# A planner's lengths for the loading queue, and the order of an even mixer's query parts

## The chip, the cores and the metric

The kernel runs on one core of a Trainium2 chip. Its engines are TensorE (PE; its weight loads are shown apart as PEld), VectorE (DVE), ScalarE (ACT), GpSimd (POOL) and SyncE (SP), which here does nothing but issue DMA transfers. The metric is the device time of one execution in microseconds (us), as the median over runs.

## The reference

The program is an encoder trunk of two layers over 512 tokens of width 1024, with 256 memory tokens. Each layer has four steps, each followed by a layer norm: a half-step SwiGLU FFN, a token mixer, cross attention into the memory, and a second FFN.

```python
for i in range(DEPTH):
    j = i // 2
    y = swiglu(x, ffn_w_gate[i, 0], ffn_w_up[i, 0], ffn_w_down[i, 0])
    x = layer_norm(ALPHA * x + 0.5 * y, ln_g[i, 0], ln_b[i, 0])
    if i % 2 == 0:
        y = mixer_ab(x, ab_w_in[j], ab_w_out[j], ab_q_gain[j], ab_k_gain[j], ab_sink[j], ang_2d, ang_1d)
    else:
        y = mixer_c(x, c_w_in[j], c_w_out[j], c_rpb[j])
    x = layer_norm(ALPHA * x + y, ln_g[i, 1], ln_b[i, 1])
    y = memory_attn(x, mem, mem_w_q[i], mem_w_kv[i], mem_w_o[i])
    x = layer_norm(ALPHA * x + y, ln_g[i, 2], ln_b[i, 2])
    y = swiglu(x, ffn_w_gate[i, 1], ffn_w_up[i, 1], ffn_w_down[i, 1])
    x = layer_norm(ALPHA * x + 0.5 * y, ln_g[i, 3], ln_b[i, 3])
```

The even mixer (layer 0) has eight heads of dense attention with rms-normed, rotated queries and keys, and eight heads of attention in a window of 128 tokens to either side, with a learned sink. Heads are 64 wide, and four query heads share a key head. The odd mixer (layer 1) has 16 heads of attention in a two-dimensional neighbourhood with a bias per offset. Everything is float32.

## The kernel before

**Products.** Float32 operands are split in two parts of a narrower type (`fp32r`): a high part, which ScalarE makes as a cast, and a low part, which VectorE makes as the operand minus the high part. A product is three matmuls into one PSUM bank: high by high, high by low, low by high. So nearly everything that TensorE takes needs one ScalarE and one VectorE instruction first, in this order. Weights come through `weights`: SP loads them into one of two `raw` buffers, then the two engines split them into `slab` buffers. A third load into `raw` has to wait until the first buffer has been split.

**What sets the order.** The class `Graph` does not issue instructions as the program calls them. `record` stores each call as an `Op` with what it depends on. `emit` then plans twice: `plan` is a list scheduler over a model of the five engines and of two DMA queues (SP's and POOL's), with a cost in ns for each instruction (`cost`) and a length for each transfer. The first pass takes ready instructions in the order in which they were recorded. `deadlines` goes back through that order and gives every DVE, ACT and POOL instruction a due time; the second pass takes those as keys, while PE and SP keep the recorded rank. The instructions are issued in the order of the second pass, and on the chip each engine works through its own in that order, waiting where an operand isn't there. The model's times are thus not the chip's; they decide only who stands before whom. Since one length in the model changes the time of everything that follows, a changed length can swap instructions far from any transfer.

In the model a transfer on SP begins 1200 ns after its issue has ended, and not before the one ahead of it has ended; it takes 1650 ns for each 512 KB. A PSUM bank is held by one engine at a time in the model, reads included (`info["bank"]` in `record`).

**The even mixer's queries.** `queries` turns the queries of a pair of heads so that features lie on partitions, in one bank `ps`: partitions 0 to 63 are the one head, 64 to 127 the other. Each head's operand is a buffer of 128 partitions whose one half holds the high part and whose other half the low part. So a pair needs two ACT instructions (high parts) and two DVE instructions (low parts), each on 64 partitions; they are recorded ACT, DVE, ACT, DVE, and stand in the order of one instruction each for the pairs.

**The even mixer's end.** The output weights `ab_w_out` are loaded in `w_rows_pairs`, as two transfers to 64 partitions each. The last two loads (raw_1107 and raw_1112) take whole rows. The second of them goes into the `raw` buffer that held the memory tokens (raw_1080, from `memory_tokens`, called after head 13 of 16), which are split into four `slab` buffers for the memory attention that follows.

**The odd mixer.** Scores of a pair of heads are matmuls on a buffer `slab` that holds high and low parts of two heads; SP copies the parts there from `t2` buffers (four transfers of 128 KB for each buffer: two with high parts, two with low parts). PE interleaves the scores (`a`) with the values times probabilities of the pair before (`d`).

In names such as slab_1086_1167 below, the first number counts buffers through the program; the texts name a buffer by it. All instructions have the line of the call in `Op` (L156, and L157 after the change); a profile names buffers without numbers.

## Time and profile before

| | us |
|---|---|
| median of 3 runs (lowest to highest) | 2132.85 (2131.11 to 2132.93) |
| the profiled execution, whole | 2131.03 |
| its span, from the first to the last instruction | 2129.3 |
| PE busy | 2112.0 (99%) |
| PEld busy | 1870.6 (88%) |
| DVE busy | 1735.8 (82%) |
| ACT busy | 1161.7 (55%) |
| POOL busy | 285.1 (13%) |
| mean granted TensorE clock | 0.998 |

Outside the span lie 1.73 us of the profiled execution, and it is 1.82 us under the median. A busy time is the sum of an engine's instructions; matmuls overlap, since the end of one is modelled and the next has already begun, so a PE that is shown as 99% busy can still start its matmuls some tenths late. Whether it does is seen in the distance between starts. In a timeline a row is a run of like instructions: its start, its time to the end of the last, engine, line, operation, what it writes and reads, its shape, how many there are, and in square brackets how long the engine had been idle before it and what ended that. In the chain, each piece is what the next had to wait for.

### The profile page before, as it was taken

What the parts mean: (1) busy time and instruction counts of PE and PEld (TensorE: products, weight loads), DVE (VectorE), ACT (ScalarE), POOL (GpSimd) and SP (SyncE); (2) the same over time, 40 slices, a digit from 0 to 9 for tenths busy, and PEclk for the clock granted to TensorE, in tenths of its full rate; (3) what the DMA queues carried; (4) which work ended last, traced back from release to release, by engine and by line L of the source; (5) the groups of instructions that cost most, each with busy time, mean ns of one, the idle gap of its engine ahead of it and who ended that gap; (6) DMA issues with size and microseconds to landing.
All of it is one profiled execution on the core that took longest, in us unless ns stands there. A gap on an engine that the chain in (4) does not pass through costs nothing.

```text
span 2129.3 us, 32714 instructions
## 1 busy us (share of the span) xinstructions
PE 2112.0 (99%) x12648; PEld 1870.6 (88%) x12648; DVE 1735.8 (82%) x2500; ACT 1161.7 (55%) x1903; POOL 285.1 (13%) x379
## 2 busy tenths in 40 slices
PE   9999999999999999999999999999999999999997
PEld 7999988888888899998889999888888888999996
DVE  7789989888848879998879999866568479699997
ACT  5555443798546554445545455457665465444552
POOL 0001015310002000000200000312210011000003
PEclk9999999999999999999999999999999999999999
DMA  6566562003433346564445556256454433456551
GB/s 204 143 165 140 139 191 91 20 18 106 140 134 109 88 114 185 150 157 130 140 106 141 129 139 187 76 149 160 118 164 157 139 91 98 109 149 155 141 151 60
DMA packets 208859, 275.92 MB, mean 130 GB/s; under 512 B 10688, under 2 KB 151616, under 8 KB 208704
## 3 DMA queue, kind: packets, MB, share of 16 engines
q1 hardware_dynamic: 175904, 221.14, 33.6%
q0 software_dynamic: 32512, 52.44, 14.0%
q8 instruction: 100, 1.64, 0.3%
q14 instruction: 55, 0.45, 0.1%
q10 hardware_dynamic: 288, 0.26, 0.0%
HBM read 259.12 MB, written 4.19 MB: 124 GB/s over the span
## 4 chain that ended last, share of the span: by engine, by line
PE 89%; DVE 1%; DMA 1%; ACT 1%; issue 1%; SPq 0%; DVEq 0%; POOL 0%; ACTq 0%
PE a L156 55%; PE d L156 21%; PE t L156 14%; DMA slab<-t 1%; ACT slab L156 1%; DVE slab L156 1%; SPq L156 0%; DVE x L156 0%; ACT t L156 0%; DMA raw<-ab_w_out 0%; DVE t L156 0%; DVE xl L156 0%; DVEq L1657 0%; ACT xh L156 0%; DVE nmu L156 0%
## 5 line engine op out<-in xcount | busy, mean ns | idle before, releaser
L156 DVE TENSOR_TENSOR slab<-slab,slab 128x1024 fp32r<-128x1024 f32 (+3 forms) x638 | 727.9, 1167 | 76.0 <-ACT slab L156 37.7
L156 ACT CAST slab<-slab 128x1024 fp32r<-128x1024 f32 (+2 forms) x498 | 472.1, 983 | 341.4 <-DVE slab L156 142.7
L156 PE MATMUL a<-slab,slab 128*128 128x256 f32 (+3 forms) x2320 | 567.6, 323 | 1.9 <-DMA slab<-t 1.2
L156 PE MATMUL a<-xh,slab 128*128 128x256 f32 (+2 forms) x2480 | 559.8, 315 | 0.1
L156 PE MATMUL d<-slab,slab 128*128 128x512 f32 (+2 forms) x1856 | 447.8, 381 | 0.8 <-DVE slab L156 0.8
L156 PEld LDWEIGHTS a<-slab,slab 128*128 128x128 f32 x2320 | 409.4, 190 | 41.7 <-ACT t L156 1.3
L156 PEld LDWEIGHTS a<-xh,slab 128*128 128x128 f32 x2480 | 416.4, 190 | 33.4 <-ACT slab L156 1.0
L156 PE MATMUL a<-raw,slab 128*128 128x256 f32 x2048 | 388.8, 283 | 1.1 <-DVE t L156 1.0
L156 PE MATMUL a<-xl,slab 128*128 128x256 f32 (+1 forms) x1240 | 389.7, 314 | 0.0
L156 PEld LDWEIGHTS d<-slab,slab 128*128 128x128 f32 x1856 | 328.9, 189 | 57.2 <-DVE slab L156 1.7
L156 PEld LDWEIGHTS a<-raw,slab 128*128 128x128 f32 x2048 | 327.8, 192 | 6.7 <-ACT slab L156 1.9
L156 PEld LDWEIGHTS a<-xl,slab 128*128 128x128 f32 x1240 | 236.3, 191 | 18.4
L156 PE MATMUL t<-slab,slab 128*128 128x512 f32 (+1 forms) x840 | 209.3, 389 | 0.0
L156 DVE TENSOR_TENSOR slab<-raw,slab 128x1024 fp32r<-128x1024 f32 (+2 forms) x140 | 159.6, 1157 | 23.3 <-ACT slab L156 23.2
L156 PEld LDWEIGHTS t<-slab,slab 128*128 128x128 f32 x840 | 149.9, 189 | 26.2
L156 DVE TENSOR_TENSOR slab<-t,slab 128x512 fp32r<-128x512 f32 (+2 forms) x223 | 137.5, 637 | 12.3 <-ACT slab L156 11.2
L156 ACT CAST slab<-t 128x512 fp32r<-128x512 f32 (+2 forms) x223 | 120.7, 567 | 41.4 <-DVE t L156 15.0
L156 ACT CAST slab<-raw 128x1024 fp32r<-128x1024 f32 (+1 forms) x132 | 123.7, 970 | 25.1 <-PE a L156 9.0
L156 ACT COPY t<-a 128x512 f32<-128x512 f32 (+1 forms) x116 | 63.5, 551 | 130.0 <-PE a L156 76.5
L156 DVE SCALAR_TENSOR_TENSOR x<-d,x 128x512 f32<-128x512 f32 x168 | 114.9, 686 | 16.8 <-PE d L156 16.1
L156 POOL DMA_DIRECT2D slab<-ffn_w_down x40 | 47.7, 1193 | 315.2 <-DVE slab L156 296.9
L156 DVE TENSOR_TENSOR t<-a,t 128x512 f32<-128x512 f32 (+2 forms) x99 | 61.0, 618 | 33.8 <-PE a L156 20.6
(126 smaller groups left out, 2143.0 us busy)
## 6 DMA issues: line engine op xcount, KB each, us to landing
slab<-ffn_w_gate SPq DMA_DIRECT2D x80, 512.0 KB
slab<-ffn_w_up SPq DMA_DIRECT2D x80, 512.0 KB
slab<-ffn_w_down SPq DMA_DIRECT2D x80, 512.0 KB
slab<-ffn_w_down POOLq DMA_DIRECT2D x40, 512.0 KB, 5.8
raw<-mem_w_kv SPq DMA_DIRECT2D x16, 1024.0 KB
slab<-t SPq DMA_DIRECT2D x96, 128.0 KB
slab<-ffn_w_gate POOLq DMA_DIRECT2D x16, 512.0 KB, 7.7
slab<-ffn_w_up POOLq DMA_DIRECT2D x16, 512.0 KB, 6.0
```

The lines of the kernel that those rows point to most:

```text
L156: op.call = lambda: fn(*args, **kw)
```

## The change

Two things are changed, both only in what the planner is told. First, the length of a transfer on SP's queue is now 250 ns and 1700 ns for each 512 KB (1950 for a transfer of 512 KB, where it was 1650), it begins 1040 ns after its issue has begun (where it was 1200 ns after the end of an issue of 600, so 1800), and it takes 1.7 times as long if it moves 512 KB or more into 64 partitions or fewer. That last case is only the two loads of `ab_w_out` in whole rows, four transfers of 512 KB. POOL's queue is as it was. Second, `queries` records both ACT parts and then both DVE parts, and the first DVE part depends on the second ACT part, so that the planner puts them in that order.

```diff
--- before.py
+++ after.py
@@ -40,7 +40,7 @@
 
 class Op:
     __slots__ = (
-        "engine", "adds", "ns", "call", "deps", "users", "wait", "ready", "end", "frees", "index", "rank", "dma", "size", "port", "table",
+        "engine", "adds", "ns", "call", "deps", "users", "wait", "ready", "end", "frees", "index", "rank", "dma", "size", "port", "table", "thin",
         "key", "start", "stop", "lands", "later",
     )
 
@@ -149,6 +149,7 @@
         func = args[2] if method == "activation" else None
         op.table = str(func) if func in (AF.Silu, AF.Exp) else None
         op.size = math.prod(outs[0].shape) * 4
+        op.thin = op.dma and engine == "sync" and op.size >= 2**19 and outs[0].shape[0] <= 64
         op.port = method in ("tensor_tensor", "scalar_tensor_tensor", "tensor_scalar") and (
             engine == "gpsimd" or engine == "vector" and math.prod(outs[0].shape[1:]) >= 64 and all(z.space != bass.MemoryType.PSUM for z in ins)
         )
@@ -254,8 +255,9 @@
             lands = stop + self.LATENCY[e]
             if op.dma:
                 kind = e == "sync"
-                work = op.size / 2**19 * (4000.0 if op.adds else 1650.0)
-                begin = max(stop + (1200.0 if kind else 2000.0), queues[kind][-1][1])
+                work = 250.0 + op.size / 2**19 * 1700.0 if kind else op.size / 2**19 * (4000.0 if op.adds else 1650.0)
+                work *= 1.7 if op.thin else 1.0
+                begin = max(t + 1040.0 if kind else stop + 2000.0, queues[kind][-1][1])
                 finish = begin + work + 0.5 * shared(queues[not kind][-6:], begin, begin + work)
                 queues[kind].append((begin, finish))
                 lands = finish + 790.0
@@ -1060,15 +1062,18 @@
             n = len(blocks) * P
             ps = self.transposed([(i * P, P, tiles[t][:, pr * P : (pr + 1) * P]) for i, t in enumerate(blocks)])
             both = both or self.pair()
-            for s, z in enumerate(both):
-                z = z[:, blocks[0] * P : blocks[0] * P + n]
-                own, other = slice(64 * s, 64 * s + 64), slice(64 - 64 * s, 128 - 64 * s)
-                shape = lambda y: y.rearrange("p (r c) -> p r c", r=ROWS) if natural else y
-                src = by_rows(ps[own, :n], natural)
-                nc.scalar.activation(shape(z[own]), src, AF.Copy, scale=-0.125)
+            own = lambda s: slice(64 * s, 64 * s + 64)
+            shape = lambda y: y.rearrange("p (r c) -> p r c", r=ROWS) if natural else y
+            src = [by_rows(ps[own(s), :n], natural) for s in range(2)]
+            z = [z[:, blocks[0] * P : blocks[0] * P + n] for z in both]
+            for s in range(2):
+                nc.scalar.activation(shape(z[s][own(s)]), src[s], AF.Copy, scale=-0.125)
+            for s in range(2):
                 nc.vector.scalar_tensor_tensor(
-                    out=shape(z[other]), in0=src, scalar=-0.125, in1=shape(z[own].bitcast(F32)), op0=ALU.mult, op1=ALU.subtract
+                    out=shape(z[s][own(1 - s)]), in0=src[s], scalar=-0.125, in1=shape(z[s][own(s)].bitcast(F32)),
+                    op0=ALU.mult, op1=ALU.subtract,
                 )
+            nc.ops[-2].deps.add(nc.ops[-3])
             return both
 
         def keys(tile_, natural):
```

No instruction, operand or buffer is added or taken away. Each engine has the same instructions in another order: about 100 of ACT's rows, 140 of DVE's and of PE's, 6 of POOL's and two pairs of SP's stand elsewhere. Of the even mixer's query parts both ACT instructions now stand together, and both DVE instructions behind them. Three other places follow.

ScalarE in the even mixer near its end. The rows `ACTIVATE t2,l<-t2,mn` are exponentials of scores, `ACTIVATE t2<-t2,l` the division by their sums, slab_1086 to slab_1092 the high parts of turned probabilities, and slab_1081 to slab_1084 those of the memory tokens raw_1080. Before:

```order
L156 ACTIVATE t2_1045_1126<-t2_1045_1126,l_1047_1128 128x384
L156 ACTIVATE t2_1049_1130<-t2_1049_1130,l_1051_1132 128x256
L156 ACTIVATE t2_1067_1148,l_1069_1150<-t2_1067_1148,mn_1068_1149 128x385
L156 ACTIVATE t2_1063_1144,l_1065_1146<-t2_1063_1144,mn_1064_1145 128x257
L156 CAST slab_1086_1167<-t_1085_1166 128x256
L156 CAST slab_1088_1169<-t_1087_1168 128x384
L156 CAST slab_1090_1171<-t_1089_1170 128x384
L156 ACTIVATE t2_1071_1152,l_1073_1154<-t2_1071_1152,mn_1072_1153 128x385
L156 CAST slab_1092_1173<-t_1091_1172 128x256
L156 CAST slab_1081_1162<-raw_1080_1161 128x2x256
L156 CAST slab_1082_1163<-raw_1080_1161 128x2x256
L156 CAST slab_1083_1164<-raw_1080_1161 128x2x256
```

After:

```order
L157 ACTIVATE t2_1049_1130<-t2_1049_1130,l_1051_1132 128x256
L157 CAST slab_1083_1164<-raw_1080_1161 128x2x256
L157 CAST slab_1084_1165<-raw_1080_1161 128x2x256
L157 CAST slab_1081_1162<-raw_1080_1161 128x2x256
L157 CAST slab_1082_1163<-raw_1080_1161 128x2x256
L157 CAST slab_1086_1167<-t_1085_1166 128x256
L157 CAST slab_1088_1169<-t_1087_1168 128x384
L157 CAST slab_1090_1171<-t_1089_1170 128x384
L157 ACTIVATE t2_1067_1148,l_1069_1150<-t2_1067_1148,mn_1068_1149 128x385
L157 CAST slab_1092_1173<-t_1091_1172 128x256
L157 ACTIVATE t2_1063_1144,l_1065_1146<-t2_1063_1144,mn_1064_1145 128x257
L157 ACTIVATE t2_1071_1152,l_1073_1154<-t2_1071_1152,mn_1072_1153 128x385
```

The four casts of the memory tokens now stand ahead of the casts of turned probabilities and of the three exponentials; VectorE's subtractions for them move ahead in the same way, between those for slab_1086 and slab_1088.

TensorE at the even mixer's output projection. d_1118 and a_1119 are two of its sums and d_1127 a third; slab_1113 and slab_1114 are the high and low part of the weights that were loaded as raw_1112. Before:

```order
L156 MATMUL d_1118_1199<-slab_1110_1191,slab_1026_1107 128x512
L156 MATMUL d_1118_1199<-slab_1113_1194,slab_1078_1159 128x512
L156 MATMUL d_1118_1199<-slab_1114_1195,slab_1078_1159 128x512
L156 MATMUL d_1118_1199<-slab_1113_1194,slab_1078_1159 128x512
L156 MATMUL d_1118_1199<-slab_1115_1196,slab_1103_1184 128x512
L156 MATMUL a_1119_1200<-slab_1111_1192,slab_1026_1107 128x512
L156 MATMUL d_1118_1199<-slab_1116_1197,slab_1103_1184 128x512
```

After:

```order
L157 MATMUL d_1118_1199<-slab_1110_1191,slab_1026_1107 128x512
L157 MATMUL d_1118_1199<-slab_1113_1194,slab_1078_1159 128x512
L157 MATMUL a_1119_1200<-slab_1111_1192,slab_1026_1107 128x512
L157 MATMUL a_1119_1200<-slab_1110_1191,slab_1026_1107 128x512
L157 MATMUL a_1119_1200<-slab_1113_1194,slab_1078_1159 128x512
L157 MATMUL d_1127_1208<-slab_1108_1189,slab_966_1047 128x512
L157 MATMUL d_1127_1208<-slab_1109_1190,slab_966_1047 128x512
L157 MATMUL d_1118_1199<-slab_1114_1195,slab_1078_1159 128x512
L157 MATMUL d_1118_1199<-slab_1113_1194,slab_1078_1159 128x512
```

Between the matmul of d_1118 on slab_1113 and the one on slab_1114 there now stand five matmuls of other sums.

TensorE in the odd mixer, at the scores of one pair of heads. a_2794 to a_2811 are banks of scores; of two matmuls into one the first reads the half of slab_2768 or slab_2769 that is copied first, the second the half that is copied second. d_2813 and d_2814 are values times probabilities, t_2824 the next product. Before:

```order
L156 MATMUL d_2813_2894<-slab_2773_2854,slab_2704_2785 128x2x128 x2
L156 MATMUL a_2805_2886<-slab_2769_2850,slab_2730_2811 128x192 x2
L156 MATMUL d_2814_2895<-slab_2775_2856,slab_2703_2784 128x256
L156 MATMUL a_2807_2888<-slab_2769_2850,slab_2730_2811 128x256 x2
L156 MATMUL d_2814_2895<-slab_2775_2856,slab_2703_2784 128x256
L156 MATMUL a_2809_2890<-slab_2769_2850,slab_2730_2811 128x256 x2
L156 MATMUL a_2811_2892<-slab_2769_2850,slab_2730_2811 128x192 x2
L156 MATMUL d_2814_2895<-slab_2775_2856,slab_2703_2784 128x256 x2
L156 MATMUL d_2814_2895<-slab_2777_2858,slab_2704_2785 128x256 x2
```

After:

```order
L157 MATMUL a_2805_2886<-slab_2769_2850,slab_2730_2811 128x192
L157 MATMUL d_2814_2895<-slab_2775_2856,slab_2703_2784 128x256
L157 MATMUL d_2814_2895<-slab_2777_2858,slab_2704_2785 128x256
L157 MATMUL a_2807_2888<-slab_2769_2850,slab_2730_2811 128x256
L157 MATMUL d_2814_2895<-slab_2777_2858,slab_2704_2785 128x256
L157 MATMUL a_2809_2890<-slab_2769_2850,slab_2730_2811 128x256
L157 MATMUL d_2814_2895<-slab_2777_2858,slab_2704_2785 128x2x128 x2
L157 MATMUL t_2824_2905<-slab_2818_2899,xh_2_83 128x512
L157 MATMUL a_2805_2886<-slab_2769_2850,slab_2730_2811 128x192
L157 MATMUL a_2807_2888<-slab_2769_2850,slab_2730_2811 128x256
L157 MATMUL a_2809_2890<-slab_2769_2850,slab_2730_2811 128x256
```

The second matmuls of a_2805, a_2807 and a_2809 now stand behind the first ones of all three, five of d_2814 and one of t_2824.

## The prediction

> **What bounds the kernel now.** I read the page's first and fourth part first (busy time, and the shares of the chain that ended last), then TensorE's waits, then the timelines of the places where the order of instructions differs. Page, parts 1 and 4:
>
> ```profile
> PE 2112.0 (99%) x12648; PEld 1870.6 (88%) x12648; DVE 1735.8 (82%) x2500; ACT 1161.7 (55%) x1903; POOL 285.1 (13%) x379
> ...
> PE 89%; DVE 1%; DMA 1%; ACT 1%; issue 1%; SPq 0%; DVEq 0%; POOL 0%; ACTq 0%
> ```
>
> The reader is to see that TensorE (PE) is the bound: 2112.0 of 2129.3 us, and 89% of the chain. No matmul is added or removed, so a new order can only give back time in which PE waits, or add such time. How much there is to give back stands in PE's waits, total us, times, longest:
>
> ```profile
> PE a L156 <- DMA slab<-t: 1.2, 3, 0.6
> PE t L156 <- DVE junk L156: 1.2, 1, 1.2
> PE a L156 <- DVE t L156: 1.0, 1, 1.0
> PE d L156 <- DVE slab L156: 0.8, 1, 0.8
> PE t L156 <- DVE x L156: 0.6, 1, 0.6
> ```
>
> These are the large ones; they come to 4.8 us. The row "DVE junk" is the start, and "DVE t" sits in the first FFN at 129 us, where the order is the same in both kernels; "DVE x" is the layer norm before the odd mixer, also unchanged. What the change can reach is the first row (the odd mixer's scores, which wait for copied query and key parts) and the fourth (one matmul in the even mixer's output projection). This view counts idle time after a matmul's modelled end. I therefore price a wait by starts: two starts on PE less the slot of the first. The slot is 0.23 us for 512 columns and 0.12 for 256, by these timeline rows (start, us busy; a row with x7 is seven matmuls from that start):
>
> ```profile
> 1049.39 0.39 PE L156 MATMUL a<-slab,xl 128*128 128x512 f32 x1
> 1049.62 0.39 PE L156 MATMUL a<-slab,xh 128*128 128x512 f32 x1
> ...
> 1528.67 1.02 PE L156 MATMUL d<-slab,slab 128*128 128x256 f32 x7
> 1529.53 0.25 PE L156 MATMUL a<-slab,slab 128*128 128x192 f32 x1
> 1530.38 0.33 PE L156 MATMUL a<-slab,slab 128*128 128x192 f32 x1 [0.60 <-DMA slab<-t]
> ```
>
> (1049.62 − 1049.39 = 0.23; (1529.53 − 1528.67)/7 = 0.12.)
>
> **Term 1, the late output weights of the even mixer (−1.0 us).** Rows of the chain, SP, ACT, DVE and PE timelines, in this order:
>
> ```profile
> 519.92 6.59 DMA raw<-ab_w_out
> ...
> 519.28 1.25 SPq L156 DMA_DIRECT2D raw<-ab_w_out  x2
> ...
> 526.61 2.00 ACT L156 CAST slab<-raw 128x1024 fp32r<-128x1024 f32 x2 [1.98 <-DMA raw<-ab_w_out]
> ...
> 527.70 2.36 DVE L156 TENSOR_TENSOR slab<-raw,slab 128x1024 fp32r<-128x1024 f32 x2 [1.50 <-ACT slab L156]
> ...
> 526.80 1.41 PE L156 MATMUL d<-slab,slab 128*128 128x512 f32 x5
> 528.98 0.50 PE L156 MATMUL d<-slab,slab 128*128 128x512 f32 x1 [0.76 <-DVE slab L156]
> ...
> 516.08 2.19 ACT L156 CAST slab<-raw 128x512 fp32r<-128x512 f32 x4
> ...
> 516.75 2.50 DVE L156 TENSOR_TENSOR slab<-raw,slab 128x512 fp32r<-128x512 f32 x4
> ```
>
> The buffer of raw_1112 is free only when DVE has split the memory tokens raw_1080 (516.75 + 2.50 = 519.25); SP issues the load at once (519.28), it lands 6.59 us after the second issue, ACT casts, DVE subtracts, and PE waits for that split: the last of the five starts at 526.80 + 4 × 0.23 = 527.72, the next matmul at 528.98, so 1.26 − 0.23 = 1.0 us are lost. Now the four casts stand right behind the last normalisation of the head before (512.77, see term 2). Each takes 0.52 of the queue (2.19 with the tail of the last), so they run from about 512.8 to 514.9, and the subtractions, between other work of DVE, are through near 517.0. The load is issued some 2.2 us earlier and lands near 524.3. Beside that PE has five other matmuls (5 × 0.23 = 1.15) between the one on the cast part and the one on the subtracted part. Either of the two covers the 1.0. Ends: −1.0 and 0; I take −1.0, since two covers would both have to fail.
>
> The Trainium skill ("SBUF — State Buffer", section "Door 1: The DMA port swizzle") gives 196 GB/s for a 1 MiB load into 64 partitions against 328 for 128. By that this load, which comes as two halves of 64 partitions, would take 1.05 MB / 196 GB/s = 5.4 us (an estimate), land 1.2 us sooner than the row shows, and PE would not wait for it even before; term 1 would be 0 and the sum 1.0 us smaller. The trace has 6.59 and the wait, so the measurement decides.
>
> **Term 2, what the earlier casts push back (+0.3).**
>
> ```profile
> 511.75 1.02 ACT L156 ACTIVATE t<-t,l 128x384 f32<-128x384 f32 x2
> 512.66 0.61 ACT L156 ACTIVATE t<-t,mn 128x385 f32<-128x385 f32 x1
> ...
> 514.14 1.19 ACT L156 CAST slab<-t 128x256 fp32r<-128x256 f32 x3 [0.28 <-PE t L156]
> ...
> 514.57 0.85 PE L156 MATMUL d<-slab,slab 128*128 128x256 f32 x3
> ```
>
> Behind those casts on ACT now stand the casts of the turned probabilities (slab_1086, 1088, 1090; before at 514.14) and the exponentials of the next heads (before at 512.66). The first cast ends about 4 × 0.52 + 0.37 after 512.7, at 515.1. PE wants it at 514.57, or at 514.80 now that one other matmul stands ahead: +0.3. The later parts have 0.2 to 0.3 us of room, since PE's new order puts three, then five matmuls of d_1094 between them. The exponentials end near 518.3 instead of 518.7, because ACT has the same work and only another order. Ends: 0, and +0.6 if the casts take 2.19 + 0.5.
>
> **Term 3, the odd mixer's scores (−1.2).** PE's timeline at two other places like the one at 1530.38 above:
>
> ```profile
> 1482.30 0.28 PE L156 MATMUL d<-slab,slab 128*128 128x256 f32 x1
> 1482.86 0.58 PE L156 MATMUL a<-slab,slab 128*128 128x192 f32 x3 [0.28 <-DMA slab<-t]
> ...
> 1484.61 0.39 PE L156 MATMUL t<-slab,xh 128*128 128x512 f32 x1
> 1485.10 0.33 PE L156 MATMUL a<-slab,slab 128*128 128x192 f32 x1
> ...
> 1551.95 0.30 PE L156 MATMUL d<-slab,slab 128*128 128x256 f32 x1
> 1552.28 0.33 PE L156 MATMUL a<-slab,slab 128*128 128x192 f32 x1
> 1552.90 0.33 PE L156 MATMUL a<-slab,slab 128*128 128x192 f32 x1 [0.30 <-DMA slab<-t]
> ```
>
> Lost: 1482.86 − 1482.30 − 0.12 = 0.44 and 1485.10 − 1484.61 − 0.23 = 0.26; 1530.38 − 1529.53 − 0.12 = 0.73; 0.33 − 0.12 = 0.21 and 0.62 − 0.12 = 0.50. The copies are issued by SP in the same order as before, so I leave their landings where they are and move only PE. At 1530 eight other matmuls (five of d_2814, two scores on the first half, one of the next product) now stand between the matmul on the first half and that on the second, which PE reaches at 1531.1, after the landing: −0.73. At 1552 three matmuls of 0.12 stand there: 0.50 becomes 0.14, −0.36. At 1482 the second halves stand directly behind the first ones, one matmul earlier than before: PE reaches them at 1482.23 and waits 0.63, after which nothing else is late: 0.63 instead of 0.70, −0.1. Sum −1.2; ends −1.5 (all of 1552 too) and 0.
>
> **Edits that I cost at nothing.** The query parts themselves: ACT's and DVE's rows of one of them.
>
> ```profile
> 402.47 0.58 ACT L156 ACTIVATE slab<-t 64x512 fp32r<-64x512 f32 x1
> ...
> 404.50 0.59 ACT L156 ACTIVATE slab<-t 64x512 fp32r<-64x512 f32 x1
> ...
> 403.79 0.68 DVE L156 SCALAR_TENSOR_TENSOR slab<-t,slab 64x512 fp32r<-64x512 f32 x1
> ...
> 405.15 0.69 DVE L156 SCALAR_TENSOR_TENSOR slab<-t,slab 64x512 fp32r<-64x512 f32 x1
> ```
>
> The second ACT part started 0.03 after DVE's first ended (403.79 + 0.68 = 404.47), so the four are done one after the other, 3.4 us from 402.47 to 405.84. Two behind two, they could be done in 2 × 0.58 + 2 × 0.68 = 2.5. PE's waits above have no row of 1 us or more on such a part, so other matmuls cover most of the chain, and shortening it by 3.4 − 2.5 = 0.9 gains a part of that at best: 0, ends −0.3 and +0.3 (a third of the 0.9, gained, or lost where another value is pushed behind a part).
>
> In the rms norm of the first query block the transpose of slab_532 moves up on PE from 376.39 to about 374.6, and POOL's addition that it needs took 373.43 to 375.82:
>
> ```profile
> 373.43 2.39 POOL L156 TENSOR_TENSOR slab<-t,t 128x512 f32<-128x512 f32 x1 [1.30 <-DVE t L156]
> ...
> 376.39 0.27 PE L156 MATMUL t<-ident,slab 128*128 128x128 f32 x1
> ```
>
> POOL waited 1.30 us there for DVE, whose rope work for this block now stands ahead of others, so I take 0; ends 0 and +1.2.
>
> At the start of the second layer's first FFN PE takes six matmuls on slab_1949 from 1049.85 on, 4.1 us before DVE had made it (1052.69 + 1.22 = 1053.91); but DVE too now makes it before the addition that stood at 1045.96:
>
> ```profile
> 1045.96 0.69 DVE L156 SCALAR_TENSOR_TENSOR x<-d,x 128x512 f32<-128x512 f32 x1
> ...
> 1052.69 1.22 DVE L156 TENSOR_TENSOR slab<-slab,slab 128x1024 fp32r<-128x1024 f32 x1
> ```
>
> There it starts by about 1046.4 and ends by 1047.6, 2.2 us ahead of PE; the addition behind it waits anyway, for sums that PE now ends 1.1 us later. 0. The two SP swaps (FFN weights near 18 and 830 us) and the casts that trade places inside the FFN bodies lie beside work that PE has queued, with no PE wait in those rows: 0, ends ±0.3 together.
>
> **Sum.** −1.0 + 0.3 − 1.2 = −1.9 against the profiled execution: 2131.03 − 1.9 = 2129.1 (span 2127.4). The profiled execution stands 1.8 under the median 2132.85, so as a median 2130.9. A change of 0.2% is 4.3 us, about what a measurement of this kernel can tell from no change; the forecast is well inside it.
>
> **Rivals.** (a) The waits come back one step later: PE reaches the next scores earlier and waits there for copies that have not moved. For it: DMA landings set these waits, not PE. Against: the copies of the next pair hang on products that PE then also makes earlier. It gives −1.9 + 1.2 + about 0.7, so 2132.8, no change. (b) The change does nothing that reaches PE, for instance because the earlier load meets other traffic and the PE fillers only shift the wait: 2132.5 to 2133.5, as in (a). (c) Slower: DVE comes late to slab_1949. One held instruction ahead of it on DVE that makes it end after 1049.85, so more than 2.2 us late, stops PE; at worst, with DVE as in the old order, it costs 4.06, and from 1.9 on the kernel is slower: 2132.85 − 1.9 + 4.06 = 2135.0. Against it: the instructions ahead of it wait for sums that PE ends by 1045.5. (d) Much faster, over 4.3 us: all of the rows above that the change can reach, 1.0 + 2.1, do not come to that, so only waits that I have not priced could.
>
> **How the numbers follow.** Forecast (−0.5 to −3.4) 0.56; (a) and (b) 0.16; (c) and other new waits of 1 to 4 us net 0.11; new waits of over 4.3 us net 0.08; (d) 0.09. The forecast's own range is 2129.5 to 2132.3. The range for 8 in 10 reaches to (c), 2135.0, and at the low side to −4.5, where the unpriced ends of every term meet (−1.0 − 1.5 − 0.3 − 0.3 and a run to run scatter of 1.8): 2128.4. Faster by over 0.2% is (d) and a little of the forecast's tail, 0.10; slower by over 0.2% is the new waits of over 4.3 us and a little of (c), 0.10; within 0.2% is 0.80.
>
> **What would show it.** Right: raw<-ab_w_out issued near 517 instead of 519.28, no PE row with DVE slab at 528, the PE wait on DMA slab<-t down from 1.2 to about 0.5 with the one at 1482 left, and a wait of 0.3 near 514.9. Wrong: a PE wait of over 1 us on DVE slab near 1050, on POOL slab near 375, or on ACT t near 519 to 521.

## The result, and the profile after

The changed kernel takes 2125.8 us (median of 7 runs, 2125.5 to 2127.03), the kernel before beside it 2132.05 (7 runs, 2130.44 to 2132.93): a ratio of 0.9973, 95% interval 0.9963 to 0.9982. By the ratio that is 5.8 us (3.8 to 7.9), where 1.9 were forecast, and the time lies below the range (from 2128.4 us). Ratios here and below are worked out from all runs, so what they give in us can differ by some tenths from the difference of two medians. The profiled execution took 2125.8 us, with a span of 2123.9 at the same granted clock (0.998).

The page of the changed kernel, busy times and the shares of the chain that ended last:

```profile
PE 2109.2 (99%) x12648; PEld 1871.0 (88%) x12648; DVE 1735.8 (82%) x2500; ACT 1161.2 (55%) x1903; POOL 287.4 (14%) x379
...
PE 96%; DVE 1%; ACT 1%; DMA 1%; issue 0%; SPq 0%; DVEq 0%; ACTq 0%
```

All engines do the same work as before; the chain now runs over PE for 96% of the span, where it was 89%. PE's waits (total us, times, longest):

```profile
PE t L157 <- DVE junk L157: 1.2, 1, 1.2
PE t L157 <- DVE x L157: 0.7, 1, 0.7
PE t L157 <- DVE slab L157: 0.4, 1, 0.4
PE a L157 <- DMA slab<-t: 0.4, 2, 0.2
PE a L157 <- DVE slab L157: 0.4, 1, 0.4
PE a L157 <- ACT slab L157: 0.3, 1, 0.3
```

Against the waits of before, four rows are gone or smaller: "DVE t" (1.0, the first FFN), "d <- DVE slab" (0.8, the output projection), "ACT t" (0.3, the even mixer) and "DMA slab<-t" (1.2, now 0.4; the three of before are gone, and two of 0.2 are new, at 1457.78 and 1570.75). They come to 2.9 us. Two rows are new: "t <- DVE slab" (0.4, at 485.87) and "ACT slab" (0.3, at 4.90). The rest of the gain is not in this view, since it counts only idle time after a modelled end.

So the two traces are compared by starts: the same instructions of PE at both ends of a stretch, at points where PE has done the same set of work in both. Each number is the length of that stretch after less its length before, in us; a second pair of traces of both kernels, taken later on one chip, stands beside it.

| stretch of before's trace | first pair | second pair |
|---|---|---|
| 1 to 30, first loads | −0.08 | −0.70 |
| 110 to 131, first FFN | −0.90 | −1.27 |
| 131 to 455 | −0.02 | −0.05 |
| 455 to 465, even mixer | −0.52 | −0.56 |
| 465 to 526 | +0.14 | +0.13 |
| 526 to 535, output projection | −1.49 | −1.52 |
| 535 to 1035 | +0.12 | −0.07 |
| 1035 to 1075, second layer's first FFN | −0.22 | −0.23 |
| 1075 to 1457 | −0.06 | −0.05 |
| 1457 to 1580, odd mixer | −1.93 | −1.79 |
| 1580 to 2118 | −0.27 | −0.48 |
| all | −5.2 | −6.6 |

There is no single place. Four stretches carry 4.8 of the 5.2 us in the first pair and 5.1 of the 6.6 in the second: the first FFN, one point of the even mixer, the output projection and the odd mixer.

**Output projection.** Rows of the changed kernel's timelines of SP, ACT, DVE and PE, in this order:

```profile
515.52 1.25 SPq L157 DMA_DIRECT2D raw<-ab_w_out  x2
...
511.03 2.17 ACT L157 CAST slab<-raw 128x512 fp32r<-128x512 f32 x4
...
523.09 2.00 ACT L157 CAST slab<-raw 128x1024 fp32r<-128x1024 f32 x2 [0.18 <-DMA raw<-ab_w_out]
...
524.36 0.68 DVE L157 SCALAR_TENSOR_TENSOR x<-d,x 128x512 f32<-128x512 f32 x1
524.96 2.35 DVE L157 TENSOR_TENSOR slab<-raw,slab 128x1024 fp32r<-128x1024 f32 x2
...
526.48 0.84 PE L157 MATMUL a<-slab,slab 128*128 128x512 f32 x3
527.15 1.30 PE L157 MATMUL d<-slab,slab 128*128 128x512 f32 x5
```

PE goes through without a wait. This part of the trace stands 1.3 us earlier than in before, for what was gained ahead of it; the load is issued 3.8 us earlier on the clock (519.28 to 515.52), so 2.4 earlier in its place, where 2.2 were forecast. Note the row at 524.36, DVE's addition ahead of the two subtractions; it turns out to matter.

**First FFN.** Before, DVE and PE:

```profile
113.81 1.23 DVE L156 TENSOR_TENSOR slab<-slab,slab 128x1024 f32<-128x1024 f32 x1 [1.49 <-DMA slab<-ffn_w_down]
114.95 0.69 DVE L156 TENSOR_TENSOR slab<-t,t 128x512 f32<-128x512 f32 x1
...
123.15 2.96 DVE L156 TENSOR_TENSOR slab<-slab,slab 128x1024 fp32r<-128x1024 f32 x3 [0.20 <-ACT slab L156]
...
129.80 0.36 PE L156 MATMUL a<-raw,slab 128*128 128x256 f32 x1 [1.03 <-DVE t L156]
```

After, DVE:

```profile
112.96 0.68 DVE L157 TENSOR_TENSOR slab<-t,t 128x512 f32<-128x512 f32 x1
113.57 1.22 DVE L157 TENSOR_TENSOR slab<-slab,slab 128x1024 f32<-128x1024 f32 x1
```

DVE waited 1.49 us for a down weight while the product behind it (114.95) was ready. Now the product stands first and fills that idle time. From there to PE's wait at 129.80 DVE's only idle time is the 0.20 us at 123.15, so what is done earlier at 113 arrives 15 us later at PE: that wait is gone.

### The profile page after: what moved, and what is told of

Its sections match the earlier page's. It is cut to its first block, busy times and chain, and to the rows that moved or that the text cites. A ratio compares the mean times of both kernels' runs of the same rounds, so it can differ in the third digit from the quotient of the medians.

```text
span 2123.9 us, 32745 instructions
## 1 busy us (share of the span) xinstructions
PE 2109.2 (99%) x12648; PEld 1871.0 (88%) x12648; DVE 1735.8 (82%) x2500; ACT 1161.2 (55%) x1903; POOL 287.4 (14%) x379
## 4 chain that ended last, share of the span: by engine, by line
PE 96%; DVE 1%; ACT 1%; DMA 1%; issue 0%; SPq 0%; DVEq 0%; ACTq 0%
PE a L157 59%; PE d L157 23%; PE t L157 15%; DVE slab L157 1%; ACT t L157 1%; DMA slab<-t 1%; DVE x L157 0%; ACT slab L157 0%; SPq L157 0%; DVE t L157 0%; DMA raw<-x_t 0%; ACT xh L157 0%; DVE mn L157 0%; DVE xl L157 0%; DVEq L1662 0%
## 5 line engine op out<-in xcount | busy, mean ns | idle before, releaser
L157 ACT ACTIVATE t<-a 128x512 f32<-128x512 f32 (+3 forms) x65 | 36.3, 559 | 89.0 <-PE a L157 89.0
```

Of the source, the lines that this page charges most:

```text
L157: op.call = lambda: fn(*args, **kw)
```

## The experiments

Most of these kernels are the kernel before with some places of the new order: the planner runs with the old lengths and the old recording, and then, engine by engine, rows are put in the order that the new kernel (or the one with the new lengths alone) has there.

```diff
+    PLACES = {"vector": [(96, (1, 0))], ...}
...
-        order = self.plan()
+        order = self.replaced(self.plan())
```

An entry is a row's number on its engine and the order of the rows from there on. "Old" is the kernel before, run beside each. Stretches are read as in the table above, against the first trace of before.

### The two halves of the change

New lengths, old recording of the query parts:

```diff
-                work = op.size / 2**19 * (4000.0 if op.adds else 1650.0)
-                begin = max(stop + (1200.0 if kind else 2000.0), queues[kind][-1][1])
+                work = 250.0 + op.size / 2**19 * 1700.0 if kind else op.size / 2**19 * (4000.0 if op.adds else 1650.0)
+                work *= 1.7 if op.thin else 1.0
+                begin = max(t + 1040.0 if kind else stop + 2000.0, queues[kind][-1][1])
```

> The planner's new lengths alone; the query parts are recorded as before. Theory P (the gain is a sum of separate waits at the places where rows changed, read as steps between the two traces): this one keeps the places at 129 us and in the odd mixer, so -0.9 at 129, -0.5 and -0.2 near 1483 to 1488, -1.0 near 1533, -0.4 near 1553, +-0.2 elsewhere, together about -3 us: 2129. Rival D (the whole run is shifted by something that is not at these places, such as the loads running better everywhere): the time would go with no step, or this half would give nothing or all 6.

2126.43 us (9 runs), old 2131.62, ratio 0.9975 (0.9965 to 0.9985), 5.2 us where about 3 were expected. By stretch: first FFN −1.25, output projection −1.43, odd mixer −2.73, and nothing at 455 to 465. The step at the output projection is here, and not with the query parts, where it was expected. Against these stands +1.0 at 1423, a wait that comes and goes in either order (see the last section).

Old lengths, the query parts recorded two and two:

```diff
+            for s in range(2):
+                nc.scalar.activation(shape(z[s][own(s)]), src[s], AF.Copy, scale=-0.125)
+            for s in range(2):
                 nc.vector.scalar_tensor_tensor(
...
+            nc.ops[-2].deps.add(nc.ops[-3])
```

> The query parts alone; lengths as before. Theory P: the places between 400 and 533 us, so -0.7 near 458 to 461, +0.2 net near 472 to 487, -1.0 at 529 and -0.4 at 532, together about -2 us: 2130; nothing at 129 or in the odd mixer. Rival D: no steps there, the time as before or as after.

2130.43 (10 runs), ratio 0.9996 (0.9987 to 1.0006). Of the steps of the changed kernel only 455 to 465 is here, −0.53, and it has a counterpart of +0.2 at 465 to 510. Before, PE waited there for exponentials; in this kernel it has other rows in the place:

```profile
458.44 0.44 PE L156 MATMUL a<-slab,slab 128*128 128x384 f32 x1 [0.30 <-ACT t L156]
```

```profile
457.79 1.12 PE L156 MATMUL a<-slab,slab 128*128 128x256 f32 x3
458.75 0.60 PE L156 MATMUL t<-ident,t 128*128 128x128 f32 x4
```

So the lengths bring nearly everything, and the query parts about 0.5 us less 0.2, at one point.

### The first FFN

> The kernel before with one pair of VectorE's rows traded, in the first FFN: the addition slab_136 ahead of the split slab_185. Theory P: VectorE has no free time from there to TensorE's wait at 129 us, and the addition fills 1.0 of its idle 1.5 us at 112.3; so TensorE's wait at 129 falls by 0.9 to 1.0 and everything after is that much earlier: -0.9 us, 2131.1. Rival: the wait at 129 differs from run to run or comes from the order of the first 30 us; then the swap gives 0.

Only DVE's two rows at 113 us, the entry shown above: 2131.01 (10 runs), ratio 0.9995 (0.9986 to 1.0005); the stretch 110 to 131 is 0.43 shorter, about half of what was expected. The trace of the change has one more pair there, two casts of ACT:

```diff
+        "scalar": [(84, (1, 0))],
+        "vector": [(96, (1, 0))],
```

> The kernel before with two pairs of rows traded in the first FFN: VectorE's slab_136 ahead of slab_185, and ScalarE's slab_192 ahead of slab_188. Theory V (between 112 and 129 us the two engines form one chain that ends in TensorE's wait at 129, and VectorE's pair alone gave 0.3 to 0.4 because ScalarE then still cast slab_188 and slab_192 in the old order): the stretch 110.0 to 131.1 is 0.8 to 1.0 us shorter, as in the changed kernel. Rival (the rest of the 0.9 came from where the weights landed in that execution): 0.3 to 0.5, as with VectorE's pair alone.

2130.98 in a single run (old 2132.28); the stretch is 0.70 shorter. Both pairs are needed for the whole of it, since with DVE's pair alone DVE's next rows wait for an ACT row that stood behind the cast of the late weight. How much it is worth depends on when loads land, and that differs from run to run: in the seven traces with both pairs the stretch is 0.17 to 1.25 shorter, in eleven others with neither it lies between 0.33 shorter and 0.08 longer. The two smallest of the seven are inside the range of the eleven: in one (0.17, the kernel with three places, below) DVE waits 2.31 us for the down weight all the same, in the other (0.29, the changed kernel without the factor, below) it was late already, for the load of the sinks:

```profile
109.78 0.17 DVE L157 TENSOR_SCALAR nsink<-nsink 128x8 f32<-128x8 f32 x1 [1.46 <-DMA nsink<-ab_sink]
```

The cause stands; its size is not fixed.

### The output projection

PE's rows alone, at the projection and in the odd mixer:

```diff
+        "tensor": [(3119, (3, 6, 7, 13, 14, 0, 1, 2, 8, 9, 4, 5, 10, 11, 12)), (8883, (4, 0, 1, 2, 3)), ...],
```

> The kernel before with TensorE's rows alone in the new order at the output projection of the even mixer (the rows at 528.5 to 533) and in the odd mixer (1476 to 1554); ScalarE, VectorE, GpSimd and SyncE as before. If the other matmuls between the two halves cover the waits (theory F): -1.0 at 529, -0.4 at 532, and in the odd mixer -0.1 to -0.5 at 1483, -1.0 at 1533, -0.4 at 1553, together -2.9 to -3.3: 2129. If the earlier load and earlier splits did it (theory E): 0 to -0.3 at 529, and in the odd mixer less than half of those steps.

2133.99 (10 runs), ratio 1.0012 (1.0002 to 1.0021): slower, which neither theory expected. The stretch 526 to 535 is 1.02 longer. Rows of this kernel, DVE and PE:

```profile
527.78 2.36 DVE L156 TENSOR_TENSOR slab<-raw,slab 128x1024 fp32r<-128x1024 f32 x2 [1.68 <-ACT slab L156]
530.06 0.68 DVE L156 SCALAR_TENSOR_TENSOR x<-d,x 128x512 f32<-128x512 f32 x1
...
530.80 1.42 PE L156 MATMUL d<-slab,slab 128*128 128x512 f32 x5 [1.80 <-DVE x L156]
```

PE does not wait here for the weights. The first two of these five matmuls are those of d_1127, and they wait for DVE's addition at 530.06, which must first read the sum that stands in their PSUM bank; that addition stands behind the two subtractions that wait for the weights. Two of the five matmuls meant as a cover thus hang on the same late load by another way.

The casts of the memory tokens alone, ACT's rows at 512.7 and DVE's at 513.4:

```diff
+        "scalar": [(470, (9, 10, 7, 8, 2, 3, 4, 0, 6, 1, 5))],
+        "vector": [(668, (10, 1, 11, 2, 8, 9, 4, 5, 7, 3, 0, 6))],
```

> The kernel before, with ScalarE's eleven rows from 512.7 and VectorE's twelve rows from 513.4 alone in the new order (the memory tokens are split first); TensorE as before. Theory E (the wait at the output projection is set by when the second load of whole rows is issued, and an earlier load alone removes it): the load is issued near 517 instead of 519.28, and the stretch 525.8 to 535.0 is 1.0 to 1.5 us shorter; against that the stretch 510.0 to 525.8 is 0.3 to 0.6 longer, since TensorE has no other matmuls ahead of the late cast. Theory B (both are needed, the earlier load and TensorE's new order): 0 to -0.5 in 525.8 to 535.0.

2136.28 in a single run (old 2132.28). The stretch 526 to 535 is 1.41 shorter (the load is issued at 517.85, with this trace 1.0 us late), but 510 to 526 is 1.48 longer: ACT now casts the turned probabilities behind the memory tokens, and PE waits for them and for their low parts:

```profile
516.18 0.85 PE L156 MATMUL d<-slab,slab 128*128 128x256 f32 x3 [0.39 <-ACT slab L156]
...
518.30 3.80 PE L156 MATMUL d<-slab,slab 128*128 128x384 f32 x18 [0.65 <-DVE slab L156]
```

The gain at the load is as expected, the loss 2.5 to 5 times as large.

What else this trace has more (first loads +1.04, 1350 to 1457 +2.4, odd mixer +1.45) lies where no row was changed.

Both together, with PE's rows at 515 to 518:

```diff
+        "tensor": [(3048, (1, 0)), (3051, (13, 14, 0, 1, 2, ...)), (3119, (3, 6, 7, 13, 14, 0, ...))],
```

> As the run on the casts, with TensorE's rows at 514.6 to 518.5 and 528.5 to 533 in the new order too. Theory E: the stretch 525.8 to 535.0 as in the run on the casts, 1.0 to 1.5 us shorter than before, and 510.0 to 525.8 within 0.2 of before. Theory B: -1.4 to -1.5 here, as in the changed kernel, where the casts alone give 0 to -0.5.

2132.07 in a single run (old 2132.28). 526 to 535 gains 0.83 and 510 to 526 loses 0.39; the gain is less than either theory had. At 526 to 535 PE still waits for DVE's addition, the bank again, since this kernel has it still behind the subtractions:

```profile
529.48 1.43 PE L156 MATMUL d<-slab,slab 128*128 128x512 f32 x5 [0.32 <-DVE x L156]
```

All engines' rows of 505 to 535:

```diff
+        "scalar": [(453, (8, 0, 1, ...)), (467, (1, 0)), (470, (9, 10, 7, ...)), ...],
+        "vector": [(654, (7, 0, 2, ...)), (666, (1, 0)), (668, (10, 1, 11, ...)), (689, (2, 0, 1))],
+        "tensor": [(3009, (2, 3, 0, 1)), (3048, (1, 0)), ...],
```

> The kernel before with the rows of all engines in the new order from 505 to 535 us, nothing else. Theory B (the gain at the output projection needs the rows of all three engines there, those around the casts included): the stretch 525.8 to 535.0 is 1.4 to 1.5 us shorter and 510.0 to 525.8 within 0.2, where the partial run gave -0.8 and +0.4. Theory Q (the rest came with the query parts from 400 us on): as in the partial run, -0.8 and +0.4.

In the trace 526 to 535 is 1.49 shorter, as in the changed kernel, and 510 to 526 is unchanged; the entry 689 is DVE's addition moved ahead. But 465 to 510 is 0.69 longer: the first entry of ACT puts an exponential ahead of four divisions that PE waits for. In the changed kernel, whose rows upstream are new too, the same entry costs at most the 0.2 there. In the times there is nothing: 2132.22 (10 runs), old 2132.31, ratio 1.0001 (0.9992 to 1.001).

The changed kernel without the factor for loads into 64 partitions:

```diff
-                work *= 1.7 if op.thin else 1.0
+                pass
```

> The changed kernel without the factor 1.7 for transfers into 64 partitions. Only rows between 513 and 557 us are then others: TensorE keeps its new order at 529, while ScalarE and VectorE split the memory tokens nearly as late as before. If the earlier split is what removes the wait: the stretch 525.8 to 535.0 is 0 to 1.0 us longer than before, as in the run with TensorE's rows alone, so 1.5 to 2.5 us of the 6 are lost: 2127.3 to 2128.3. If TensorE's other matmuls cover it: 2125.8, and 525.8 to 535.0 stays 1.4 shorter.

2128.91 (10 runs), old 2132.31, ratio 0.9983 (0.9974 to 0.9992): 3.6 us faster, so by the ratios 2.2 of the 5.8 us are missing without the factor (the two kernels were not run beside each other, and the intervals touch). The wait is back, and the load is issued as late as in before less the 1.2 us that the trace is ahead:

```profile
518.02 1.25 SPq L157 DMA_DIRECT2D raw<-ab_w_out  x2
...
527.79 0.96 PE L157 MATMUL d<-slab,slab 128*128 128x512 f32 x3 [0.76 <-DVE slab L157]
```

526 to 535 takes what it took in before (+0.01): 1.5 us stand here, and what else is missing has no place: the other stretches that are longer in this trace (110 to 131, and 1355 to 1435) have the changed kernel's rows. One multiplication, for four transfers of the whole program, is what moved the casts.

The place once more, with all engines' rows of 512 to 535 as the new lengths alone order them:

```diff
+        "scalar": [(470, (7, 8, 9, 2, 3, 4, 10, 6, 0, 1, 5)), (489, (1, 0)), (496, (1, 0))],
+        "vector": [(668, (8, 1, 2, 4, 5, 9, 10, 11, 7, 3, 0, 6)), (689, (2, 0, 1))],
+        "tensor": [(3062, (2, 3, 4, ...)), (3075, (1, 0)), (3083, (1, 0)), (3097, (2, 0, 1)), (3118, (4, 7, 14, ...))],
```

> The output projection's place alone, with the rows of 512 to 535 us as the new lengths order them on all engines; the earlier run of this place also moved rows of 503 to 512 us and lost 0.66 us on them. Theory: -1.4 us at 526 to 535 and 0 before it, ratio 0.9992 to 0.9996. Rival (the place gains nothing in the times, whatever its trace shows, because a later wait gives it back): 1.0000.

526 to 535 gains 1.46, and 535 to 560 gives back 0.87:

```profile
537.76 1.09 PE L156 MATMUL t<-ident,x 128*128 128x128 f32 x8 [0.64 <-DVE x L156]
```

These are the turns of the first block after the layer norm; PE comes to them earlier, DVE and POOL don't have the norm ready. Times: 2131.82 (11 runs), ratio 0.9999 (0.999 to 1.0008), as the rival had it. With the rows behind it, up to 570 us, in the new order too:

```diff
+        "tensor": [..., (3155, (8, 9, 10, 11, 0, 1, 2, 3, 4, 5, 6, 7)), ...],
+        "scalar": [..., (500, (1, 0)), (507, (4, 2, 3, 0, 1)), (515, (1, 2, 3, 0)), (521, (1, 0))],
+        "vector": [..., (698, (1, 2, 3, 4, 6, 5, 7, 12, 9, 10, 11, 0, 8)), ...],
```

> The output projection's place alone with those rows behind it (512 to 570 us). Theory: -1.4 us at 526 to 535 and no wait at 537.5, 1.0 to 1.5 us faster, ratio 0.9991 to 0.9997. Rival (given back elsewhere): 1.0000, as for the place without the rows behind it (0.9999).

```profile
536.49 0.85 PE L156 MATMUL d<-slab,slab 128*128 128x512 f32 x3
537.18 1.03 PE L156 MATMUL t<-ident,x 128*128 128x128 f32 x8
```

PE has three more products ahead of the turns and no wait: 535 to 560 at −0.02, 526 to 535 at −1.46. That much was expected and is seen. The times are 2131.59 (11 runs), ratio 0.9999 (0.999 to 1.0007), the rival's number: at most 2.1 us faster, which leaves room for the 1.4 but does not show it.

### The odd mixer

All engines' rows of 1400 to 1600:

```diff
+        "tensor": [(8577, (1, 0)), (8587, (1, 0)), (8589, (1, 0)), (8883, (4, 0, 1, 2, 3)), ...],
+        "scalar": [(1161, (4, 0, 1, 2, 3)), ...], "vector": [(1589, (1, 2, 3, 0)), ...], "gpsimd": [(243, (1, 0)), ...], "sync": [(295, (1, 0))],
```

> The kernel before with the rows of all engines in the new order from 1400 to 1600 us, nothing else. Theory B (TensorE's order and the other engines' order are needed together, since either alone gave nothing): 1479.9 to 1490.0 is 0.7 to 0.8 us shorter, 1515.0 to 1540.0 0.8, 1539.9 to 1558.0 0.5 to 0.8, and 1456.9 to 1580.0 together about 1.9 to 2.7 shorter, where kernels with the old order read between -1.0 and +0.6; the median falls by 2, to 2129.6. Rival (the shorter waits of the changed kernel come from where the copies and loads fell after earlier places had moved): -1 or less.

2131.46 (11 runs), ratio 0.9996 (0.9987 to 1.0005). The stretch 1457 to 1580 is 0.84 shorter, where about 1.9 to 2.7 were expected; by its number the rival holds, so the rows of this place alone do not carry the odd mixer's whole step. The kernel with PE's rows alone (above) is 0.17 longer there: it gained 0.4 to 0.6 at each of three waits for copies, at 1483, 1533 and 1553, and lost about 0.6, 0.6 and 0.3 in new ones at 1482, 1506 and 1553. The opposite, all engines but PE (with rows of 451 to 459 too):

```diff
+        "scalar": [(353, (1, 0)), (359, (3, 0, 1, 2)), (1161, (4, 0, 1, 2, 3)), ...],
+        "vector": [(540, (1, 2, 0)), (543, (2, 0, 1)), ..., (1650, (2, 0, 1)), ...],
+        "gpsimd": [(255, (1, 0)), ...],
```

> The kernel before with the rows of all engines but TensorE in the new order at 451 to 459 (even mixer) and at 1460 to 1560 (odd mixer). Even mixer: if the exponential that fills ScalarE's idle time is the whole of it, the stretch 455.0 to 465.0 is 0.5 us shorter. Odd mixer, where TensorE's rows alone gained nothing: theory N (the other engines' order makes the parts that are copied earlier, and that is what the odd mixer gains): 1480 to 1490 is 0.5 to 0.8 shorter and 1515 to 1540 0.4 to 0.8. Theory B (both are needed): within 0.4 of the kernels with the old order, which read -0.1 to +0.3 and -0.5 to 0 there.

2133.7 in a single run (old 2132.28), the stretch 1.51 longer. At 451 to 459 the wait came at 453 instead of 458 (+0.65 and −0.65 on the two sides of 455). So neither half does it alone, at either place.

The old order itself varies in this stretch. In ten more traces that have it on all engines, 1457 to 1580 lies from −0.67 to +0.47 against the first, and once (the casts alone) at +1.45. Seven have the new order: −0.28, −0.84, −1.00 where only places are new, −1.93, −2.16, −2.42 and −2.73 where the whole plan is. The new order of the whole plan is better, the places alone are not clear of the old order's range, and one trace sizes the step only to about 1 us.

### The places together

The first FFN, the output projection (512 to 535) and the odd mixer, all engines, as the new lengths order them; and the complement, everything of the new lengths' order but these:

```diff
+        "scalar": [(84, (1, 0)), (470, (7, 8, 9, ...)), ..., (1335, (4, 0, 1, 2, 3))],
+        "vector": [(96, (1, 0)), (668, (8, 1, 2, ...)), ..., (1800, (4, 0, 1, 2, 3))],
+        "tensor": [(3062, (2, 3, 4, ...)), ..., (9507, (4, 0, 1, 2, 3))],
...
+        "tensor": [(9, (1, 3, 0, 2)), (33, (2, 0, 3, 5, 1, 4)), ...],
+        "scalar": [(16, (1, 0)), (19, (1, 0)), ...],
```

> The old kernel with the new planner lengths' order at three places only, on all engines: the first FFN (the two pairs upstream of the wait at 129 us), the output projection (rows of 512 to 535 us) and the odd mixer (rows of 1400 to 1600 us). Theory (the gain is three waits at these places, and the other new rows do nothing): it comes near the run with the new lengths everywhere, which was 5.2 us faster (ratio 0.9975, 0.9965 to 0.9985): 4 to 5.5 us, ratio 0.9974 to 0.9981, and in the trace steps of about -0.9, -1.45 and -1.9 us. Rival (the single places gained 1.3, 0.1 and 0.9 us in the times, so most of the gain lies in rows that no run has moved alone, or in the first two microseconds of order elsewhere): 2 to 2.5 us, ratio 0.9988 to 0.9991.

> The complement: the old kernel with the new lengths' order everywhere but at those three places. Theory: no change, ratio 0.9995 to 1.0005 (0 to 0.3 us from the start of the second layer's first FFN). Rival: 2.5 to 3 us faster, ratio 0.9986 to 0.9988.

Three places: 2129.21 (11 runs), old 2131.97, ratio 0.999 (0.9982 to 0.9999), which is 2.1 us by the ratio and 2.8 by the medians. The rest: 2133.42 (11 runs), ratio 1.0006 (0.9997 to 1.0015), 1.3 us to the slow side. For the three places the rival has the number, but not the reason: the rest should then have gained 2.5 to 3 us, and it gains nothing. So the shares don't add up to the lengths' 5.2: a place seems to be worth less where its neighbours are in the old order. One such loss is seen in the trace, +0.97 at 537 (that trace is of the slowest of the 11 runs, 2132.29); with the rows up to 570 us:

> The three places, but with the rows behind the output projection (to 570 us: the layer norm's transposes and the first products of the next block) also as the new lengths order them. Theory (the three places lost part of their gain to rows behind them that were still in the old order: +0.9 at 537.5, where PE's transposes wait for the layer norm): 0.9 us more than the run with three places, 3.7 us faster in all, ratio 0.9978 to 0.9987. If the new lengths' whole 5.2 us is there too (0.9971 to 0.9979), nothing but these places matters; if it stays at 2.8 us (0.9985 to 0.9992), the row at 537.5 is not what was given back.

2129.13 (11 runs), old 2132.17, ratio 0.9986 (0.9977 to 0.9995), 3.0 us (1.1 to 4.9). The wait at 537 is gone in the trace (535 to 560 at −0.01). Whether the times gained by it can't be told: 0.9 us more by the ratios, as expected, 0.3 by the medians, both inside the intervals. Three places with their rows behind carry about 3 of the 5.2 us. Where the other 2 come from is not settled: the intervals of this run and of the lengths alone meet (0.9977 to 0.9995, 0.9965 to 0.9985), and the traces put much of the difference on waits for DMA landings. One of them, at the first scores of the last pair of heads, where both kernels' rows stand in the same order; before, SP's copies and PE:

```profile
1567.31 5.16 SPq L156 DMA_DIRECT2D slab<-t  x8
...
1573.13 1.33 PE L156 MATMUL a<-slab,slab 128*128 128x512 f32 x7
```

Three places and the rows behind:

```profile
1564.79 5.22 SPq L156 DMA_DIRECT2D slab<-t  x8
...
1572.36 0.58 PE L156 MATMUL a<-slab,slab 128*128 128x192 f32 x3 [0.57 <-DMA slab<-t]
```

Before, PE went through its last dense products and these scores in one piece that was over 7.15 us after SP's first issue (1573.13 + 1.33 − 1567.31). In the other execution it waited for a copy until 7.57 us after it. Landings differ from run to run, but that need not be all: the stretch 1558 to 1580 is 0.74 to 1.27 longer in the three traces where only places are new, and between 0.03 shorter and 0.42 longer in the four where the whole plan is.

### Second traces of both kernels

> The kernel before, unchanged, for a second trace beside a second one of the changed kernel on one chip. Theory (places recur, landings don't): against the first trace of the same kernel PE's steps are within 0.1 us at 458 to 461, 526 to 535 and 537, and up to 1 us apart where PE waits for a DMA (the first 30 us, 110 to 131, the odd mixer). The subtraction near 1362 takes 2.4 or 3.6 us, whichever the chip makes it take. Rival (the steps of 0.5 to 1.5 us are themselves run to run): differences of that size at 458 and 526 too.

> The changed kernel, unchanged, on the same chip. Theory: against the kernel before on this chip -0.5 at 458 to 461, -1.5 at 526 to 535, 0 at 535 to 560, -0.2 at 1035 to 1075, and in sum -0.5 to -1.3 at 110 to 131 and -1.5 to -3 in the odd mixer, 5 to 6.5 us in all. The subtraction near 1362 takes what it takes in the kernel before on this chip (theory: it belongs to the chip); rival: it belongs to the order, and takes 2.4 here as in the first trace while the kernel before has 3.6.

2131.42 (8 runs) and 2126.1 (8 runs), old 2131.57: ratios 0.9999 (0.9987 to 1.001) and 0.9974 (0.9963 to 0.9985). The second pair is in the table at the top. The steps at 455 to 465, 526 to 535 and 1035 to 1075 recur within 0.04 us. In the kernel before alone, the two traces are 0.57, 0.35 and 0.31 apart at 1515 to 1540, 1540 to 1558 and 1480 to 1490, and 0.56 apart in the first 30 us, all with the same order: that is scatter from run to run, at places where PE waits for loads and copies.

## Why the prediction was wrong

**The frame held.** PE is the bound, only its waits can be given back, and the wait at the output projection went away by the step that was named: earlier casts, an earlier load. The failure is in the count of the waits.

**"DVE t sits in the first FFN at 129 us, where the order is the same in both kernels": wrong, 0.9 to 1.3 us.** The order at 129 us is the same; the order at 113 us is not, and DVE had almost no idle time between (0.2). A wait was judged by the rows at its own place, when its cause was the last idle time of the engine that it names. Rival (d), "only waits that I have not priced could", came true, by this row among others.

From the −1.9 of the sum to the −5.2 of the first pair of traces, this row is −0.9, term 1 −0.5, term 2 −0.35, term 3 −0.7, the query parts −0.3 and the second layer's first FFN −0.2; what is left lies in the first loads and at the end. The range was added up wrongly at its low end: the terms that it names come to −4.9 and not −4.5, so to 2128.0 us, and the result lies below that too.

**Term 1, −1.0 forecast, −1.5 measured (1.49 and 1.52).** The load moved as reckoned. The loss was sized too small: matmuls behind the wait also started late. PE's rows of before:

```profile
528.98 0.98 PE L156 MATMUL d<-slab,slab 128*128 128x512 f32 x3 [0.76 <-DVE slab L156]
529.79 0.40 PE L156 MATMUL a<-slab,slab 128*128 128x512 f32 x1
530.11 0.73 PE L156 MATMUL d<-slab,slab 128*128 128x512 f32 x2
530.68 0.62 PE L156 MATMUL a<-slab,slab 128*128 128x512 f32 x2
```

Six matmuls from 528.98 to 530.68 take 1.70, against 6 × 0.23 = 1.38: another 0.3. And "either of the two covers the 1.0" is false for PE's five matmuls: alone they made the stretch 1.0 longer, and in the changed kernel without the factor they stand there and the wait is back. The earlier casts do cover it alone (−1.41), but gave 1.48 back at 516, where term 2 has 0.3. The whole 1.5 without a loss came only with the other rows of the place, among them one that the prediction doesn't name, DVE's addition ahead of the subtractions, which sets the bank of d_1127 free.

The Trainium skill's figure for a load into 64 partitions ("SBUF — State Buffer", section "Door 1: The DMA port swizzle"), by which term 1 would have been 0, does not hold here: the load took 6.59 us where the estimate from that figure was 5.4, the wait was there, and taking it away gave 1.5 us.

**Term 2, +0.3 forecast, −0.05 measured.** In the changed kernel PE's rows at 515 move with the casts (19 matmuls in one piece from 514.58) and there is no wait near 514.9. Where only some of the rows there were moved the cost was +0.39, and with none of PE's +1.48; so the mechanism is real and the cover was better than reckoned.

**Term 3, −1.2 forecast, −1.9 and −1.8 measured, but with about 1 us of scatter.** The step that failed is "move only PE": with PE's rows alone the stretch is 0.17 longer, since what it gained at three waits it lost in new ones, for copies (0.42 at 1483.58) and for DVE (0.38 at 1507.98). With all rows the steps at 1533 and 1553 are about −0.9 and −0.5 (−0.73 and −0.36 were forecast), but at 1553 traces of the old order alone differ by that much (1540 to 1558 from 0.01 to 0.55 shorter than the first). The wait at 1482, which was to stay, went too. Here "I leave their landings where they are" failed: SP's four copies took 3.27 us from the first issue to the end of the last in before and 2.38 in the changed kernel, in the same order of SP. Rows of before, of the changed kernel, of the second trace of before and of the kernel with all engines' new rows but PE's, in this order:

```profile
1482.77 3.27 SPq L156 DMA_DIRECT2D slab<-t  x4
```

```profile
1479.47 2.38 SPq L157 DMA_DIRECT2D slab<-t  x4
```

```profile
1483.29 3.10 SPq L156 DMA_DIRECT2D slab<-t  x4
```

```profile
1483.98 2.38 SPq L156 DMA_DIRECT2D slab<-t  x4
```

In the twelve traces with the old rows of ACT, DVE and POOL there the four take 2.47 to 3.54 us, in the eight with the new ones 2.38 to 2.79; mostly it is the second pair of copies that starts later behind the first. In all seven traces with every engine's new rows 1480 to 1490 is 0.61 to 0.81 shorter than in the first trace, in ten more with the old ones between 0.29 shorter and 1.16 longer. So this step belongs to the change: the other engines' new order lets SP issue the copies sooner.

**Edits costed at nothing.** The query parts gave 0.5 at 458 and lost 0.2 behind it, inside the ±0.3 that they were given; the sign and the mechanism (PE's wait on an exponential, not on a query part) were not foreseen. The second layer's first FFN gave 0.2. The transpose at 374 gave nothing, as taken, and rivals (b) and (c) did not come.

**Rival (a)**, the waits that come back a step later, is what the kernels with single places do (at 530.8 behind PE's rows alone, at 537.8 behind the projection). In the changed kernel, whose plan is new everywhere, it is small (the new wait of 0.44 at 485.87). The prediction priced places one by one, as those kernels move them, and that is the wrong unit for a planner's change.

## What to carry to other kernels

Price a wait at the last idle time of the engine that it names, not at its own place: an engine that is busy for 15 us in between hands the delay on. A filler put ahead of a late operand is a cover only if its own bank and operands don't hang on the same late row. A new order from a planner works as a whole; a part of it, moved alone, can gain at its place and give back behind it, so what its parts gain alone need not add up to what it gains.

## What was not expected of the hardware

**A subtraction of DVE beside POOL's additions takes 2.4 or 3.64 us, with the rows there in the same order.** At 1362 us DVE subtracts 128x1024 while POOL adds 128x512 blocks; POOL started 2.50 us ahead both times. DVE and POOL of the kernel before, and of the changed one without the factor:

```profile
1362.64 2.40 DVE L156 TENSOR_TENSOR slab<-slab,slab 128x1024 fp32r<-128x1024 f32 x1
...
1360.14 9.01 POOL L156 TENSOR_TENSOR x<-x,slab 128x512 f32<-128x512 f32 x6
```

```profile
1361.31 3.64 DVE L157 TENSOR_TENSOR slab<-slab,slab 128x1024 fp32r<-128x1024 f32 x1
...
1358.81 5.05 POOL L157 TENSOR_TENSOR x<-x,slab 128x512 f32<-128x512 f32 x4
```

Alone, a subtraction of this shape takes 1.22 (the row at 113.57 above). POOL's additions start 1.25 us apart, so the third starts at 1362.64 and at 1361.31, in the same hundredth as DVE's subtraction. 2.40 is 1.22 and about one addition, 3.64 is 1.22 and two: DVE waits out POOL's third addition or also the fourth. In the first case the fourth takes 2.32 (it waits for DVE), in the second 1.30, and PE loses 1.2 us at 1366. The Trainium skill says that the two engines take a shared port as a lock for a whole instruction and the loser waits ("SBUF — State Buffer", section "Who interferes with whom"); the trace agrees, and it adds that the lock was not always handed over after one instruction. It was 3.64 in 9 traces and 2.4 in 11; kernels run one after the other on a chip agreed, and one chip gave either value at different times. What decides it is open. The four traces of the table at the top all have 2.4, nine of the experiments' traces have 3.64.

**A wait at 1423 us comes and goes in either order.** There, at scores of the odd mixer, PE waits in some traces, by the view for copies or for DVE, and not in others. The stretch 1415 to 1435 is 1.18 longer than in the first trace in the kernel with the casts alone, whose rows there are the old ones, 1.13 in the changed kernel without the factor and 1.01 with the lengths alone; the second trace of before and both of the changed kernel are 0.10 to 0.13 shorter. A single trace that has this wait reads 1 us slower for it. What decides it is open.
